# Other steps for the returns, the residual's columns, the stores and the bias tiles of an attention block, and two small moves in its opening and in its FFN

## The chip, the cores and the metric

The kernel runs on one core of a Trainium2 chip. The metric is the device time of one execution in microseconds (us). Of the kernel before, three runs were timed: 2106.54, 2106.32 and 2105.35 us, median 2106.32. One more execution was taken by the hardware profiler; the times inside the program are from it, counted from its first instruction.

## The reference, cut to what matters

One layer of a decoder on 512 tokens of width 2048, all in float32: a norm, an attention mixer, an added residual, a norm, a SwiGLU network, an added residual, a last norm.

```python
def rmsnorm(x, g):
    y = x32 * lax.rsqrt(jnp.mean(x32 * x32, axis=-1, keepdims=True) + RMS_EPS)
    return (y * g.astype(jnp.float32)).astype(x.dtype)

def nsa_mixer(h, ...):                       # 16 heads of 128 in 4 groups
    q, kc, vc, ks, vs, kw, vw, gl = jnp.split(h @ w_in, bounds, axis=-1)
    # o_c: attention on compressed keys (31 blocks), with the bias of a table by distance
    # o_s: attention on the selected blocks;  o_w: attention in a window of 512, same bias
    o = (gates[:, :, 0, :, :, None] * o_c + gates[:, :, 1, :, :, None] * o_s
         + gates[:, :, 2, :, :, None] * o_w)
    return o.reshape(Bsz, S, N_HEADS * DH) @ w_out

def swiglu(h, w_in, w_out):
    z = h @ w_in
    return (jax.nn.silu(z[..., :D_FF]) * z[..., D_FF:]) @ w_out      # D_FF = 5632

h = x
h = h + nsa_mixer(rmsnorm(h, mix_norm_g), ...)
h = h + swiglu(rmsnorm(h, ffn_norm_g), ffn_w_in, ffn_w_out)
return rmsnorm(h, final_norm_g)
```

## The kernel before, in words

**Products.** A float32 product is made of three products of a faster type, fp32r: each operand is split into a high part (a copy on ACT, the scalar engine) and a low part (a subtraction on DVE, the vector engine), and `three()` issues high·high, low·high and high·low on PE, the TensorE (lines 275 to 277). Weights come from memory into one of three `raw` buffers and are split into `whi` (L94, ACT) and `wlo` (L97, DVE).

**Opening** (0 to about 45 us). x comes in, is transposed on PE and split; the first products of the keys' weights run in four passes q = 0 to 3. The row factors of the norm (1/rms of each token) stand on a diagonal matrix `diag`; a product of an all-ones matrix with it (L516, plain float32) spreads them over all partitions, and the result scales what the projections made (`ybc`). In pass q = 0, DVE also makes sixteen small copies within `tab`, the table of biases (L498), from which POOL (GpSimd) later stores `d_c` and loads `biasc`.

**Heads** (about 200 to 710 us). A loop over h from −1 to 15 runs a stream of projections on PE, `dense()`, step by step: 32 steps for each head up to 11, 36 for heads 12 to 15. Between the steps stand events, each with a place in a table of numbers: the scores of the next head for four blocks of queries (L789 on DVE, exponentials L791 on ACT, the divisor L796 and L797 on DVE, the scaling L799 on ACT), the transposes (L804), their way through memory (`d_p`, then the `pt` fetches on SP's queue, L811), the splits of what comes back (part_hi on ACT, L831; part_lo on DVE, L845 and L847), and the products with the values (`o`). At the end of a head `fold` (L873) and `whole` (L877) add the last block, and `out_hi` (L886) and `out_lo` (L893) make the head's output. Each engine carries out its own instructions in the order in which the program gives them, so the table's numbers set the order on each engine, and an instruction that waits holds up all behind it on its engine or queue.

**Spilled heads.** The outputs of heads 0 to 10 are stored to memory (`d_o`, 256 KB each, from a `stage` buffer) at the end of their head. They come back in head iterations 11 and 12: `reload_o` (L728, SP's queue), `back_hi` (L731, ACT) and `back_lo` (L734, DVE). BACK holds the step of each reload, 9.2 + 2.7 e for the e-th; the split's halves stand 9 and 9.8 steps later. Values of 32 and more belong to iteration 12 and count from its start, in its steps (36 of them to 32 numbers).

**Partial products.** In iterations 12 to 15 the stream makes six partial products of the output projection, over heads 0 to 11, for 256 columns each: `partial(cb)`, 24 steps. It takes three blocks of weights (`W.take`, eight steps each; a take also issues the load of a later block, 512 KB, on POOL's queue, where it waits for a free `raw` buffer). The columns of x, 512 KB, are loaded into `stage` on POOL's queue (L739) at the start of the partial; at the end of steps 20 and 24 DVE adds the product's two halves to them (L752), and POOL stores the sum (`d_h`, L754).

**FFN** (from about 740 us). Blocks of the activations come back from memory: `load_form` (L1339) loads the parts from which seven combinations of a block are made, `load_a` loads blocks for the plain products (`rawx`, L1249), both on SP's queue.

Of the kernel before, what the change touches and what calls it, by code (L numbers as in the profile page):

```python
# [10 lines left out]
F32 = mybir.dt.float32  # L11
F32R = mybir.dt.float32r
# [8 lines left out]
NT, KC = S // 128, D // 128  # L21
# [158 lines left out]
def nsa_block(ctx: ExitStack, tc: tile.TileContext, x, rel_bias, mix_g, ffn_g, fin_g, w_in, w_out,  # L180
              pos_k, w1k, w2k, pos_v, w1v, w2v, f_in, f_out, onehot, out):
    nc = tc.nc
    mm, act, dve, pool = nc.tensor.matmul, nc.scalar.activation, nc.vector, nc.gpsimd
# [21 lines left out]
    d_o = dram.tile([12, 128, S], F32, name="d_o")  # L205
# [88 lines left out]
    def run(gen):  # L294
        for _ in gen:
            pass

    def split_from(psum_ap, hi, lo, scale=None):
        if scale is None:
            act(hi, psum_ap, AF.Copy)  # L300
            dve.tensor_tensor(lo, psum_ap, hi.bitcast(F32), op=OP.subtract)
        else:
            act(hi, psum_ap, AF.Copy, scale=scale)
            dve.scalar_tensor_tensor(lo, psum_ap, scale, hi.bitcast(F32), op0=OP.mult, op1=OP.subtract)
# [53 lines left out]
    with ExitStack() as st1:  # L358
# [11 lines left out]
        with ExitStack() as st0:  # L370
            xp = st0.enter_context(tc.tile_pool(name="xp", bufs=1))
# [5 lines left out]
            oh = xp.tile([NB + 1, UL], F32R, name="oh")  # L377
            ohr = xp.tile([NB + 1, UL], F32, name="ohr")
            rel_hl = [xp.tile([NB + 1, H], F32R, name=f"rel_{n}") for n in "hl"]
            ones = xp.tile([128, 128], F32, name="ones")  # L380
            diag = xp.tile([128, NT, 128], F32, name="diag")
            pool.dma_start(g16, mix_g.rearrange("o (k p) -> (o k) p", p=128))
            pool.dma_start(relt[:NB, :], rel_bias)
# [13 lines left out]
            pool.dma_start(pos[:, 1], pos_v)  # L397
            dve.memset(hn_h[:, KC - 1].bitcast(F32), 1.0)
            dve.memset(relt[NB:NB + 1, :], NEG)
            dve.memset(ones, 1.0)  # L400
            dve.memset(tab[:, UL:], NEG)

            names = iter(("tr", "mlp") * 20)
# [1 line left out]
            def bank(shape):  # L405
                return ps1.tile(shape, F32, name=next(names))
# [17 lines left out]
            def pos_turn():  # L424
                p = bank([128, 2, 32])
                for i in range(2):
                    nc.tensor.transpose(p[:, i], pos[:, i], ident[:32, :32])
                dve.tensor_copy(posT, p)

            def table(c0, c1):  # L430
                p = spare([H, 512])
                for i, r in enumerate(rel_hl):
                    mm(p[:, :c1 - c0], r, oh[:, c0:c1], start=i == 0, stop=i == 1)
                dve.tensor_copy(tab[:, c0:c1], p[:, :c1 - c0])
# [14 lines left out]
            def spare(shape):  # L449
                return ps1.tile(shape, F32, name="proj")  # L450
# [10 lines left out]
            for t in range(NT):  # L461
                if t == NT - 1:
                    p = spare([128, KC])
# [23 lines left out]
            for q in range(4):  # L487
                it = ws(ps, q, W.take(0)) if q else halves(ps)
                next(it)
                if q == 3:  # L490
                    factors()
                W.ahead(1 if q else 2)
                if q == 0:
                    for c0, c1 in ((0, 512), (512, UL)):
                        table(c0, c1)
                    pos_turn()
                    for b in range(16):
                        dve.tensor_copy(tab[:, UL + CL * b:][:, :37], tab[:, 46 - b:46 - b + 16 * 36 + 1:16])  # L498
                for i in ((0, 1), (2, 3, 4), (5, 6, 7), ())[q]:
                    square(i)  # L500
                for _ in range(4):
                    next(it)
                if q == 3:
                    W.ahead(2)
                for k in range(4 * q + 4, 4 * q + 8):
                    if q < 3:
                        chunk(k)
                    if k % 4 < 3:
                        next(it)
                run(it)  # L510
# [2 lines left out]
            for _ in range(3):  # L513
                next(kc1)
            p = bank([128, S])
            mm(p, ones, diag.rearrange("p t c -> p (t c)"), start=True, stop=True)  # L516
            act(ybc, p, AF.Copy)
            W.ahead(2)
            pool.dma_start(d_t, tab[:, :UL])
# [94 lines left out]
        for i in range(8):  # L614
# [10 lines left out]
            if i == 1:  # L625
                p = ps1.tile([128, 128], F32, name="tr")
# [27 lines left out]
        p = ps1.tile([96, G, 128], F32, name="tr")  # L654
# [8 lines left out]
    with ExitStack() as st2:  # L663
        ap_ = st2.enter_context(tc.tile_pool(name="ap", bufs=1))
# [57 lines left out]

        N_BACK = 11

        BACK = [9.2 + 2.7 * e for e in range(N_BACK)]

        def reload_o(e):
            nc.sync.dma_start(hn_l[:, e].bitcast(F32), d_o[e])  # L728
# [5 lines left out]
            dve.tensor_tensor(hn_l[:, e], hn_l[:, e].bitcast(F32), hn_h[:, e].bitcast(F32), op=OP.subtract)  # L734

        def partial(cb):
            st = ap_.tile([128, 1024], F32, name="stage").rearrange("p (t c) -> p t c", t=NT)
            c = slice(256 * cb, 256 * (cb + 1))
            pool.dma_start(st, x[:, c].rearrange("(t p) c -> p t c", p=128))  # L739
            ps = [p.rearrange("p (t c) -> p t c", t=2) for p in proj2()]  # L740
            for i in range(3):
                w = W.take()
                for t in range(NT):
                    if i == 2 and t == 2:
                        W.ahead(3)
                    for k in range(4):
                        h = 4 * i + k
                        three(ps[t // 2][:, t % 2], hn_h[:, h, tok(t)], hn_l[:, h, tok(t)], w[0][:, k], w[1][:, k],
                              h == 0 and t % 2 == 0, h == 11)
                        if h == 11 and t % 2:  # L750
                            b = t // 2
                            dve.tensor_tensor(st[:, 2 * b:2 * b + 2], st[:, 2 * b:2 * b + 2], ps[b], op=OP.add)  # L752
                            if b:
                                pool.dma_start(d_h[:, c].rearrange("(t p) c -> p t c", p=128), st)  # L754
                        if k % 2:
                            yield
# [122 lines left out]
        def out_hi(h):  # L879
            s = HS[h]  # L880
            if h < N_BACK:
                s["st"] = ap_.tile([128, 1024], F32, name="stage")[:, :S]
            f = [s["st"]] if h < N_BACK else [hn_h[:, h], hn_l[:, h]]
            s["f"] = [x.rearrange("p (t i b) -> p t i b", t=4, b=32) for x in f]
            s["o"] = s["o"].rearrange("p (i t b) -> p t i b", i=4, b=32)
            act(s["f"][0], s["o"], AF.Copy)  # L886
            if h < N_BACK:
                nc.sync.dma_start(d_o[h], s["st"])

        def out_lo(h):  # L890
            s = HS.pop(h)
# [8 lines left out]
        def steps(h):  # L900

            ev = []
            g = h + 1
            if g < H:
                for t, p in START.items():
                    p += h < 0 and t == 3
                    ev += [(p, scores, g, t), (p + 5.5, finish, g, t), (p + 8.5 - (t == 0), turn, t)]
                    if t < 3:
                        ev.append((p + 8.6 - (t == 0), fetch, t + 1))
                ev += [(p[0] + 32, f, g, 0) for p, f in ((HI, part_hi), (LO, part_lo), (VALUE, values))]  # L910
                ev.append((VALUE[0] + 33.1, fold, g))
            if h >= 0:
                ev += [(.2, load_bias, h + 2), (2.5, fetch, 0), (2.6, fetch_c)]
                for i in range(1, len(SEQ)):
                    ev += [(HI[i], part_hi, h, i), (LO[i], part_lo, h, i), (VALUE[i], values, h, i)]
                ev.append((VALUE[-1] + .5, whole, h))
                ev += [(VALUE[-1] + 1, out_hi, h), (VALUE[-1] + 2, out_lo, h)]
            for e, p in enumerate(BACK):
                for n, f in ((p, reload_o), (p + 9, back_hi), (p + 9.8, back_lo)):
                    if h == (11 if n < 32 else 12):  # L920
                        ev.append((n if n < 32 else (n - 32) * 32 / (6 * N_SPILL), f, e))
            return sorted(ev, key=lambda e: e[0])

        W.queue, W.late = pool, []
        for h in range(-1, H):
            share = 32 if h < 12 else 6 * N_SPILL
            ev = steps(h)
# [315 lines left out]
    def load_a(m):  # L1243

        for n, (home, after) in held.items():
            if after == m:
                t = tp.tile([128, 1024 if home == "rawx" else 1536], F32, name=home, bufs=1)
                a_raw[n] = t[:, :2 * S]
                nc.sync.dma_start(a_raw[n], d_a[seq[n][1]])  # L1249

    def split_a(n):
        if n in held:
            h, l = (tp.tile([128, 1600], F32R, name=f"t{x}")[:, :2 * S] for x in ("hi", "lo"))
            act(h, a_raw[n], AF.Copy)
            sub(l, a_raw.pop(n), f32(h))
            a_hl[n] = h, l
        elif n < NU - N_TAIL:
            a_hl[n] = seven[seq[n][1]] if seq[n][1] in KEPT else passing.pop(0)
        load_a(n)

    def load_tail(i):
        n = NU - N_TAIL + i
# [75 lines left out]
    def load_form(i):  # L1338
        nc.sync.dma_start(form_raw[i][:, :2], d_a[seq[forms[i]][1]].rearrange("p (n c) -> p n c", n=2))  # L1339
# [52 lines left out]
            n_visit[0] += 1  # L1392

    load_form(0)
    load_form(1)
    forming = {n: form(i) for i, n in enumerate(forms)}

# [50 lines left out]
    n, na, pending = 0, 2, None  # L1448
# [85 lines left out]
    for t in range(NT - 1):  # L1534
# [8 lines left out]
        p = known(t, 3)  # L1543
        last_columns(t, po[t], 0, 512, 3)
        send(t, factor(t, 3, p), (1,))
    t = NT - 1
# [11 lines left out]
    p = known(t, 4)  # L1558
# [4 lines left out]
    for cb, eng in ((0, nc.sync), (1, nc.scalar), (3, nc.sync), (2, nc.sync)):  # L1563
        c = slice(512 * cb, 512 * (cb + 1))
# [34 lines left out]
```

## Time and profile before

| what | value |
|---|---|
| median of three runs | 2106.32 us |
| the profiled execution's own time | 2107.27 us |
| its span, first to last instruction | 2105.5 us |
| mean granted clock of TensorE | 0.998 |
| PE busy | 2091.8 us, 99% |
| DVE, ACT, POOL busy | 1589.7, 999.9 and 142.0 us |
| PE idle at 575 to 600 us | 2.82 of 25 us |
| clock granted at 600 to 625 us | 0.93 |
| ACT waiting for d_o reloads | 4.6 us, in 2 waits |

An engine's busy time is the time in which it carried out an instruction. A timeline row gives start, length, engine, line and operation, written tile <- read tiles, and in brackets the idle time before it and what ended that. The loading of weights (PEld) overlaps with PE's products.

### The profile page before, as it was taken

How to read it: one execution, taken by the hardware profiler on the slowest of the kernel's cores; microseconds unless marked ns; L12 is line 12 of the kernel's file. 1: busy time of each engine (PE TensorE's matmuls, PEld its weight loads, DVE VectorE, ACT ScalarE, POOL GpSimd, SP SyncE). 2: the span in 40 equal slices, each digit the busy share in tenths (PEclk: the TensorE clock that was granted, in tenths of full speed). 3: DMA queues.
4: the chain of work that ended last, by engine and by line, in shares of the span. 5: the costliest groups of instructions: out<-in, count | busy, mean ns of one | idle time of the engine just before them, and what ended most of it. 6: DMA issues, size and time to landing. Idle time of an engine off the chain costs nothing.

```text
span 2105.5 us, 37607 instructions
## 1 busy us (share of the span) xinstructions
PE 2091.8 (99%) x14826; PEld 1951.9 (93%) x14826; DVE 1589.7 (75%) x2619; ACT 999.9 (47%) x1631; POOL 142.0 (7%) x230
## 2 busy tenths in 40 slices
PE   9999999999999999999999999999999999999998
PEld 7898898888989989999999999999999888999997
DVE  5565667667666467988888888888888787877776
ACT  5344666666756343444343443443434454444443
POOL 2000111111111100000000000000000000000000
PEclk9999999999999999999999999999999999999999
DMA  7555667766776753444333433443433686878884
GB/s 222 192 149 153 172 181 201 194 182 177 221 215 199 233 190 101 135 136 127 125 118 124 137 115 126 126 131 121 129 122 121 233 319 216 303 273 309 312 324 160
DMA packets 256065, 385.49 MB, mean 183 GB/s; under 512 B 27626, under 2 KB 183322, under 8 KB 255248
## 3 DMA queue, kind: packets, MB, share of 16 engines
q1 hardware_dynamic: 228832, 267.57, 40.6%
q0 software_dynamic: 26064, 113.94, 16.3%
q8 instruction: 116, 1.90, 0.4%
q10 hardware_dynamic: 992, 1.57, 0.2%
q14 instruction: 61, 0.50, 0.1%
HBM read 320.26 MB, written 68.00 MB: 184 GB/s over the span
## 4 chain that ended last, share of the span: by engine, by line
PE 94%; DMA 2%; DVE 2%; ACT 1%; issue 0%; SPq 0%; DVEq 0%; ACTq 0%
PE proj L275 14%; PE proj L276 14%; PE proj L277 14%; PE f L277 13%; PE f L275 13%; PE f L276 13%; PE pp L275 1%; PE pp L277 1%; PE pp L276 1%; DMA hn_l<-d_o 1%; PE s L277 1%; PE s L275 1%; PE s L276 1%; PE o L276 1%; PE o L277 1%; PE o L275 1%
## 5 line engine op out<-in xcount | busy, mean ns | idle before, releaser
L97 DVE TENSOR_TENSOR wlo<-raw,whi 128x1024 fp32r<-128x1024 f32 (+2 forms) x226 | 271.0, 1202 | 89.3 <-ACT whi L94 88.7
L94 ACT ACTIVATE whi<-raw 128x1024 fp32r<-128x1024 f32 (+2 forms) x226 | 233.2, 1036 | 195.7 <-DVE raw L1032 119.8
L275 PE MATMUL proj<-hn_h,whi 128*128 128x512 f32 (+1 forms) x832 | 289.1, 348 | 0.0
L276 PE MATMUL proj<-hn_l,whi 128*128 128x512 f32 (+1 forms) x832 | 287.2, 345 | 0.1
L277 PE MATMUL proj<-hn_h,wlo 128*128 128x512 f32 (+1 forms) x832 | 287.3, 345 | 0.0
L1032 DVE TENSOR_TENSOR tlo<-tt,thi 128x1536 fp32r<-128x1536 f32 (+4 forms) x161 | 197.8, 1242 | 107.7 <-ACT thi L1134 87.9
L1129 ACT ACTIVATE whi<-raw 128x1024 fp32r<-128x1024 f32 x123 | 126.1, 1057 | 292.3 <-DVE raw L1032 288.9
L277 PE MATMUL f<-hn_h,wlo 128*128 128x256 f32 x656 | 181.1, 276 | 0.0
L275 PE MATMUL f<-hn_h,whi 128*128 128x256 f32 x656 | 181.1, 276 | 0.0
L276 PE MATMUL f<-hn_l,whi 128*128 128x256 f32 x656 | 181.1, 276 | 0.0
L277 PEld LDWEIGHTS proj<-hn_h,wlo 128*128 128x128 f32 x832 | 156.2, 188 | 20.7 <-DVE wlo L97 0.2
L276 PEld LDWEIGHTS proj<-hn_l,whi 128*128 128x128 f32 x832 | 156.3, 188 | 17.8 <-DVE hn_l L417 0.5
L275 PEld LDWEIGHTS proj<-hn_h,whi 128*128 128x128 f32 x832 | 156.2, 188 | 17.0 <-issue 0.2
L277 PE MATMUL proj<-whi,hn_l 128*128 128x256 f32 (+2 forms) x568 | 163.2, 287 | 0.4 <-DVE hn_l L734 0.4
L275 PE MATMUL proj<-whi,hn_h 128*128 128x256 f32 (+2 forms) x568 | 163.1, 287 | 0.1
L276 PE MATMUL proj<-wlo,hn_h 128*128 128x256 f32 (+2 forms) x568 | 162.9, 287 | 0.0
L1134 ACT ACTIVATE thi<-tt 128x1536 fp32r<-128x1536 f32 x82 | 121.9, 1487 | 83.5 <-PE proj L276 83.4
L1032 DVE TENSOR_TENSOR wlo<-raw,whi 128x1024 fp32r<-128x1024 f32 x123 | 147.0, 1223 | 0.0
L276 PEld LDWEIGHTS f<-hn_l,whi 128*128 128x128 f32 x656 | 123.1, 188 | 0.0
L275 PEld LDWEIGHTS f<-hn_h,whi 128*128 128x128 f32 x656 | 123.1, 188 | 0.0
L277 PEld LDWEIGHTS f<-hn_h,wlo 128*128 128x128 f32 x656 | 123.1, 188 | 0.0
L275 PEld LDWEIGHTS proj<-whi,hn_h 128*128 128x128 f32 x568 | 107.2, 189 | 2.6 <-ACT hn_h L731 0.5
(378 smaller groups left out, 6225.4 us busy)
## 6 DMA issues: line engine op xcount, KB each, us to landing
raw<-in_ffn_w_in SPq DMA_DIRECT2D x135, 512.0 KB, 3.6
raw<-in_ffn_w_out SPq DMA_DIRECT2D x88, 512.0 KB, 6.1
rawx<-in_ffn_w_in SPq DMA_DIRECT2D x41, 512.0 KB, 4.8
rawx<-d_a SPq DMA_DIRECT2D x32, 512.0 KB, 5.4
ah<-d_s POOLq DMA_DIRECT2D x16, 896.0 KB, 7.2
al<-d_s POOLq DMA_DIRECT2D x16, 896.0 KB, 9.2
raw<-in_nsa_w_in POOLq DMA_DIRECT2D x24, 512.0 KB, 6.4
raw<-in_nsa_w_out POOLq DMA_DIRECT2D x24, 512.0 KB, 5.6
```

The source lines that it names most:

```text
L94: self.nc.scalar.activation(hi[:, :n], src, AF.Copy)
L97: self.nc.vector.tensor_tensor(lo[:, :n], src, hi[:, :n].bitcast(F32), op=OP.subtract)
L275: mm(o, ah, bh, start=start, stop=False, skip_group_check=True)
L276: mm(o, ah, bl, start=False, stop=False, skip_group_check=True)
L277: mm(o, al, bh, start=False, stop=stop, skip_group_check=True)
L1032: dve.tensor_tensor(o, a, b, op=OP.subtract)
L1129: act(h, r, AF.Copy)
L1134: act(h, ttf, AF.Copy)
```

## The change

What it does, piece by piece:

- Opening: `ones` becomes fp32r, `diag` is split into a high and a low part (one ACT copy, one DVE subtraction, in pass 3), and the product with the diagonal becomes two fp32r products. The sixteen copies in `tab` move from pass 0 to pass 1, behind the split of the second weights.
- Bias tiles: `load_bias` (tb, 256 KB, POOL's queue) moves from step 0.2 of a head to step 18.5.
- Spilled stores: the store of a head's output (d_o, SP's queue) moves from the end of the head to step 25.5 of the next, as `store_o`.
- Residual columns: the load of x in a partial product moves from its start to behind the second of its three takes of weights, eight steps later, and in POOL's queue behind the load that this take issues.
- Returns: the reloads' steps come from a list of their own (between 10.5 and 33, before 9.2 to 36.2), and the splits' steps too (SPLIT, between 18.6 and 42.5, before 18.2 to 45.2).
- FFN: the first `load_a(1)` moves behind `load_form(0)` on SP's queue.

```diff
-            ones = xp.tile([128, 128], F32, name="ones")
+            ones = xp.tile([128, 128], F32R, name="ones")
+            diag_hl = [xp.tile([128, NT, 128], F32R, name=f"diag_{n}") for n in "hl"]
...
                     pos_turn()
+                if q == 1:
                     for b in range(16):
                         dve.tensor_copy(tab[:, UL + CL * b:][:, :37], tab[:, 46 - b:46 - b + 16 * 36 + 1:16])
...
                 if q == 3:
                     W.ahead(2)
+                    split_from(diag, *diag_hl)
...
             p = bank([128, S])
-            mm(p, ones, diag.rearrange("p t c -> p (t c)"), start=True, stop=True)
+            for i, d in enumerate(diag_hl):
+                mm(p, ones, d.rearrange("p t c -> p (t c)"), start=i == 0, stop=i == 1)
...
-        BACK = [9.2 + 2.7 * e for e in range(N_BACK)]
+        BACK = [10.5, 12, 13.5, 17.2, 18.4, 19.6, 20.8, 25.6, 26.6, 27.6, 33]
+        SPLIT = [18.6, 19.8, 21.2, 25.8, 27, 28.2, 30.5, 34, 36, 39, 42.5]
...
         def partial(cb):
-            st = ap_.tile([128, 1024], F32, name="stage").rearrange("p (t c) -> p t c", t=NT)
             c = slice(256 * cb, 256 * (cb + 1))
-            pool.dma_start(st, x[:, c].rearrange("(t p) c -> p t c", p=128))
             ps = [p.rearrange("p (t c) -> p t c", t=2) for p in proj2()]
             for i in range(3):
                 w = W.take()
+                if i == 1:
+                    st = ap_.tile([128, 1024], F32, name="stage").rearrange("p (t c) -> p t c", t=NT)
+                    pool.dma_start(st, x[:, c].rearrange("(t p) c -> p t c", p=128))
...
             if h < N_BACK:
-                nc.sync.dma_start(d_o[h], s["st"])
+                spilled[h] = s["st"]
+
+        spilled = {}
+
+        def store_o(h):
+            nc.sync.dma_start(d_o[h], spilled.pop(h))
...
             if h >= 0:
-                ev += [(.2, load_bias, h + 2), (2.5, fetch, 0), (2.6, fetch_c)]
+                ev += [(18.5, load_bias, h + 2), (2.5, fetch, 0), (2.6, fetch_c)]
...
-            for e, p in enumerate(BACK):
-                for n, f in ((p, reload_o), (p + 9, back_hi), (p + 9.8, back_lo)):
+            if 0 < h <= N_BACK:
+                ev.append((25.5, store_o, h - 1))
+            for e, (p, q) in enumerate(zip(BACK, SPLIT)):
+                for n, f in ((p, reload_o), (q, back_hi), (q + .8, back_lo)):
...
-        load_a(n)
+        if n != 1:
+            load_a(n)
...
     load_form(0)
+    load_a(1)
     load_form(1)
```

What the tables do to the order is seen in the engines' instruction lists. First DVE at the end of head 11, from the fold to the next head's scores. L873, L877 and L893 are fold, whole and out_lo before (L879, L883 and L904 after); hn_l<-hn_l,hn_h is the low part of a returned head (L734, then L739). Before:

```order
L873 TENSOR_REDUCE p_1868<-s 128x128
L877 TENSOR_TENSOR o<-o,p_1868 128x4x32
L734 TENSOR_TENSOR hn_l<-hn_l,hn_h 128x512
L893 TENSOR_TENSOR hn_l<-o,hn_h 128x512
L327 SCALAR_TENSOR_TENSOR yt<-proj,ybc 128x512
L301 TENSOR_TENSOR ql<-yt,qh 128x512
L97 TENSOR_TENSOR wlo<-raw,whi 128x1024
L734 TENSOR_TENSOR hn_l<-hn_l,hn_h 128x512
```

After:

```order
L879 TENSOR_REDUCE p_1873<-s 128x128
L739 TENSOR_TENSOR hn_l<-hn_l,hn_h 128x512
L883 TENSOR_TENSOR o<-o,p_1873 128x4x32
L904 TENSOR_TENSOR hn_l<-o,hn_h 128x512
L327 SCALAR_TENSOR_TENSOR yt<-proj,ybc 128x512
L301 TENSOR_TENSOR ql<-yt,qh 128x512
L739 TENSOR_TENSOR hn_l<-hn_l,hn_h 128x512
L97 TENSOR_TENSOR wlo<-raw,whi 128x1024
```

A returned head's low part moved from behind whole to ahead of it, and another from behind the weights' low part to ahead of it.

Then DVE some 5 us later, from the scores of a block of queries to its divisor (L796 and L797, then L802 and L803) and the next block's scores. Before:

```order
L789 ISA p_1869,ms<-s,tb 128x16x32
L789 ISA ms 128x1
L734 TENSOR_TENSOR hn_l<-hn_l,hn_h 128x512 x2
L796 RECIPROCAL ms<-ms 128x3
L797 TENSOR_TENSOR ms<-ms,gates 128x3
L734 TENSOR_TENSOR hn_l<-hn_l,hn_h 128x512
L789 ISA p_1868,ms<-s,biasc 128x31
```

After:

```order
L795 ISA p_1874,ms<-s,tb 128x16x32
L795 ISA ms 128x1
L739 TENSOR_TENSOR hn_l<-hn_l,hn_h 128x512 x3
L802 RECIPROCAL ms<-ms 128x3
L803 TENSOR_TENSOR ms<-ms,gates 128x3
L795 ISA p_1873,ms<-s,biasc 128x31
```

Three low parts now stand ahead of the divisor, where two stood ahead and one behind.

Last, POOL's queue in iterations 12 to 14, where raw are the loads of weights, stage the columns of x, tb a bias tile and d_h the store of a partial product. Before:

```order
L739 DMA stage<-in_x 128x4x256
L673 DMA tb<-d_u 128x512
L78 DMA raw<-in_nsa_w_out 128x4x256 x3
L754 DMA d_h<-stage 128x4x256
L739 DMA stage<-in_x 128x4x256
L78 DMA raw<-in_nsa_w_out 128x4x256
L673 DMA tb<-d_u 128x512
```

After:

```order
L748 DMA stage<-in_x 128x4x256
L78 DMA raw<-in_nsa_w_out 128x4x256 x2
L677 DMA tb<-d_u 128x512
L760 DMA d_h<-stage 128x4x256
L78 DMA raw<-in_nsa_w_out 128x4x256
L748 DMA stage<-in_x 128x4x256
L78 DMA raw<-in_nsa_w_out 128x4x256 x2
```

The second load of x stands behind one more load of weights, and the bias tile ahead of the store of the partial product.

More of the change, by code (lines that the diff above doesn't have):

```diff
@@ L399, in nsa_block @@
             dve.memset(relt[NB:NB + 1, :], NEG)
-            dve.memset(ones, 1.0)
+            dve.memset(ones.bitcast(F32), 1.0)
             dve.memset(tab[:, UL:], NEG)
```

## The prediction

> **What bounds the kernel now.** I read the page first, for the busy shares, then the windows of 25 us, to find where TensorE is not busy, then waits, chain and timelines of those places. In a row of the windows stand the stretch, its length, then busy time and count of PE, PEld, DVE, ACT and POOL, the granted clock, the DMA share and GB/s.
>
> ```profile
> PE 2091.8 (99%) x14826; PEld 1951.9 (93%) x14826; DVE 1589.7 (75%) x2619; ACT 999.9 (47%) x1631; POOL 142.0 (7%) x230
> 0.00:25.00 25.00, 23.31 (x114) 18.53 (x115) 13.45 (x38) 15.39 (x26) 6.97 (x18) 1.00 0.90 295
> 575.00:600.00 25.00, 22.18 (x143) 18.90 (x141) 19.05 (x45) 17.24 (x41) 2.79 (x4) 1.00 0.88 238
> 600.00:625.00 25.00, 24.43 (x180) 23.78 (x181) 16.68 (x44) 12.41 (x33) 5.04 (x7) 0.93 0.61 200
> 1650.00:1675.00 25.00, 24.36 (x128) 20.63 (x127) 22.54 (x38) 13.79 (x20) 1.60 (x3) 1.00 0.79 280
> ```
>
> TensorE is the bound. Every window not shown has 25.00 of 25 us busy, but for the last stage; so a step moved elsewhere can only lose. The one large loss lies at 575 to 625, where heads 11 and 12 meet. Three stretches with the same work, iterations 12, 13 and 14 of the heads' loop, price it:
>
> ```profile
> 581.90:621.40 39.50, 36.26 (x265) 34.14 (x264) 28.76 (x74) 23.23 (x57) 6.35 (x9) 0.96 0.71 207
> 621.40:654.00 32.60, 32.60 (x265) 32.02 (x264) 20.48 (x59) 18.80 (x48) 5.73 (x9) 1.00 0.67 194
> ```
>
> 39.50 − 32.60 = 6.9 us. Inside iteration 12 the loss sits in one spot:
>
> ```profile
> 600.38 0.45 PE L276 MATMUL o<-pt_hl,v1h 128*128 128x256 f32 x1 [2.13 <-DVE pt_hl L845]
> 598.00:600.00 2.00, 0.25 (x3) 0.04 (x1) 0.97 (x2) 1.41 (x4) 0.00 (x0) 1.00 1.13 222
> 602.00:604.00 2.00, 2.00 (x11) 2.00 (x11) 0.10 (x1) 0.63 (x1) 0.76 (x1) 0.51 0.22 77
> ```
>
> TensorE waited 2.13 us for a low part on DVE (L845), and then ran at half clock for a while: by the 0.93 granted over 600 to 625, 0.07 × 25 = 1.7 us more. That is 3.8 of the 6.9.
>
> [...]
>
> **Returns and their splits.** Heads 0 to 10 come back from memory (the d_o reloads) and are split by ACT (L731) and DVE (L734). The waits seem to accuse the reloads: ACT lost 0.79 us at the ninth, 3.83 at the eleventh.
>
> ```profile
> 593.43 0.63 ACT L731 ACTIVATE hn_h<-hn_l 128x512 fp32r<-128x512 f32 x1 [0.79 <-DMA hn_l<-d_o]
> 593.97 1.54 ACT L799 ACTIVATE p<-p,ms 128x31 f32<-128x31 f32 x3
> 603.24 0.63 ACT L731 ACTIVATE hn_h<-hn_l 128x512 fp32r<-128x512 f32 x1 [3.83 <-DMA hn_l<-d_o]
> PE proj L277 <- DVE hn_l L734: 0.4, 2, 0.2
> ```
>
> (The last row is from the waits of TensorE at 555 to 606: total, times, longest.) The change sends the last reloads earlier, the ninth and tenth ahead of the heads' turn, the eleventh 3.2 steps sooner and so ahead of the pt fetches of step 2.5; I expect both waits to go. What that is worth is read from DVE, in whose order L845 stands:
>
> ```profile
> 592.15 1.29 DVE L734 TENSOR_TENSOR hn_l<-hn_l,hn_h 128x512 fp32r<-128x512 f32 x2 [1.50 <-ACT hn_h L731]
> 593.57 0.16 DVE L797 TENSOR_TENSOR ms<-ms,gates 128x3 f32<-128x3 f32 x1
> 599.03 0.69 DVE L734 TENSOR_TENSOR hn_l<-hn_l,hn_h 128x512 fp32r<-128x512 f32 x1 [1.81 <-ACT hn_h L731]
> 599.64 0.69 DVE L845 TENSOR_TENSOR pt_hl<-pt,pt_hl 128x512 fp32r<-128x512 f32 x1
> ```
>
> L845 waits for the L734 ahead of it, that for ACT's split (1.81), that for the exponentials ahead of it on ACT, and these for L799, which could have begun when L797 ended, at 593.73, and began at 593.97 behind the late split. So the 0.79 us held L845 back by 0.24. The 3.83 us was mostly idle: L845 had gone, and TensorE's two waits for such a split are 0.4 in all. Both together: 0.6 us.
>
> Against that, the new order puts one split's low part ahead of L877. It stood behind it, in the time in which ACT makes out_hi, and cost nothing; now its 0.6 (1.29 for two) and out_hi (0.6 for that shape on ACT, at 593.43) are paid one after the other, less the 0.1 that DVE waited: yt and the next scores come up to 1.1 later. And three low parts stand ahead of L797 where two stood: another 0.6. The split at the place just ahead of L845 stays (now the eleventh, before the tenth). So L845 would end up to 1.1 + 0.6 − 0.2 = 1.5 us later. In favour: the reloads no longer compete with the pt fetches, two splits less are left to iteration 12, and the stalls before (6.9 − 3.8 − 0.4 = 2.7 us) may shrink by about as much. I take **0**, with +1.5 as the bad end and −6.9, all of the loss, as the good one. The half clock stays in the sum, since a gap of 2 us stays.
>
> **The residual's columns (x).** The load of x (512 KB) for a partial product stood at its start; it now goes behind the first take's weights in POOL's queue. Where DVE adds it (L752), all that is behind on DVE waits with it. Partial 1 (GB/s is that of 40 slices of 618 to 634, the rows under it the DMA issues there with the time to landing):
>
> ```profile
> 620.84 0.75 POOL L739 DMA_DIRECT2D stage<-in_x  x1 [5.54 <-DMA d_h<-stage]
> 622.96 0.75 POOL L78 DMA_DIRECT2D raw<-in_nsa_w_out  x1 [1.36 <-issue]
> GB/s 412 403 424 351 332 434 426 425 302 288 257 198 162 238 280 300 341 353 210 113 228 243 197 179 220 243 302 302 210 216 288 252 168 156 113 36 184 389 297 297
> stage<-in_x POOLq DMA_DIRECT2D x1, 512.0 KB, 6.0
> tb<-d_u POOLq DMA_DIRECT2D x1, 256.0 KB, 8.7
> 628.46 0.69 DVE L752 TENSOR_TENSOR stage<-stage,proj 128x512 f32<-128x512 f32 x1 [2.66 <-PE proj L277]
> 632.35 0.69 DVE L752 TENSOR_TENSOR stage<-stage,proj 128x512 f32<-128x512 f32 x1 [0.72 <-PE proj L277]
> 634.33 0.65 DVE L845 TENSOR_TENSOR pt_hl<-pt,pt_hl 128x512 fp32r<-128x512 f32 x1
> 635.10 0.32 PE L276 MATMUL o<-pt_hl,v1h 128*128 128x256 f32 x1
> ```
>
> x would be issued at 623.7, where tb stood. If it flies 6.0 us as now, it lands at 629.7, 1.2 after it is wanted; if 8.7, like tb, at 632.4, 3.9 late. DVE can take up 0.72 (its idle before the second add) and 0.12 (634.98 to 635.10). TensorE's stall: 0.4 to 3.1; I take the middle, **+1.75**. Partial 4 stands alike:
>
> ```profile
> 688.16 0.70 POOL L78 DMA_DIRECT2D raw<-in_nsa_w_out  x1 [1.04 <-issue]
> 692.31 0.69 DVE L752 TENSOR_TENSOR stage<-stage,proj 128x512 f32<-128x512 f32 x1 [4.71 <-PE proj L277]
> 695.03 0.69 DVE L752 TENSOR_TENSOR stage<-stage,proj 128x512 f32<-128x512 f32 x1 [0.90 <-PE proj L277]
> 695.64 0.69 DVE L845 TENSOR_TENSOR pt_hl<-pt,pt_hl 128x512 fp32r<-128x512 f32 x1
> 697.67 0.28 PE L276 MATMUL o<-pt_hl,v1h 128*128 128x256 f32 x1
> ```
>
> Issued at 688.9, by 6.0 us it lands at 694.9, 2.6 late, by 8.7 at 697.6, 5.3 late; the slack is 0.90 + 1.34 = 2.24. Stall 0.4 to 3.1; no tb fetch crowds it, so nearer the low end: **+0.8**. The other four partials fall between fetch bursts: 0.
>
> [...]
>
> **The opening.** Sixteen small copies held DVE while TensorE wanted L417:
>
> ```profile
> 16.48 1.67 DVE L498 COPY tab<-tab 16x37 f32<-16x37 f32 x16
> PEld proj L276 <- DVE hn_l L417: 0.5, 1, 0.5
> 25.33 0.75 DVE L417 SCALAR_TENSOR_TENSOR hn_l<-mlp,gcol,hn_h 128x512 fp32r<-128x512 f32 x1 [2.75 <-ACT hn_h L416]
> 40.66 0.39 PE L277 MATMUL proj<-hn_h,wlo 128*128 128x512 f32 x1
> 40.89 1.02 PE L516 MATMUL mlp<-diag,ones 128*128 128x512 f32 x2
> 41.98 0.39 PE L276 MATMUL proj<-hn_l,whi 128*128 128x512 f32 x1
> ```
>
> Behind the second weights they fall into 2.75 us of DVE idleness, which hides their 1.67: **−0.4** (0.5 less what PEld hides). Without that cover they would cost the same again. The fp32 product (two rows of L516, and with one matmul behind them 40.89 to 41.98, 1.09 us) becomes two of fp32r; three matmuls at 0.23 a start (40.66 to 40.89) are 0.69: **−0.4**. The diagonal's split adds one ACT copy and one DVE subtraction of 512 columns, 0.6 to 0.7 each by the rows above, while TensorE works through the last matmuls ahead of 40.89; if it is late, up to +0.5.
>
> **The row factor, FFN.** A reload (rawx) stood ahead of the form's data (acc) on SP:
>
> ```profile
> 1652.41 0.43 DVE L1035 TENSOR_TENSOR acc<-acc 128x256 f32<-128x256 f32 x1 [0.75 <-DMA acc<-d_a]
> 1662.90 0.39 PE L277 MATMUL f<-thi,al 128*128 128x256 f32 x1 [0.64 <-DVE al L1032]
> ```
>
> With acc first, DVE's 0.75 goes and the chain down to L1032 moves up: the 0.64 and some of the next start, **−0.7** (0 if rawx, now behind, is late in its turn).
>
> **Bias tiles and spilled stores.** tb moves from step 0.2 to 18.5, the d_o store from the head's end to step 25.5 of the next; each has several us until it is wanted, and in iterations 0 to 10 TensorE never waits. Cover gone, a late store would block the stage buffer of the next head: I price it at 0, bound +1.
>
> **The sum.** The profiled execution took 2107.27 us (span 2105.5). 0 + 1.75 + 0.8 − 0.4 − 0.4 − 0.7 = +1.05, so 2108.3; that execution lies 0.95 above the runs' median of 2106.32, so **2107.4** among the runs. 0.2% (4.2 us) is about what a measurement of this kernel can tell from no change: faster is below 2102.1, slower above 2110.5.
>
> **The rivals.**
> 1. *The splits were the whole loss* (faster). Sent early and taken in one batch, they leave ACT and DVE free, the wait at L845 falls well under 2 us and the half clock stays away. For it: no other iteration loses anything, and what iteration 12 has beyond 13 is the splits. Against: four of them still stand there, one just ahead of L845. −6.9 − 1.5 = 2106.3 − 8.4 = 2097.9; without the half clock alone, −1.7 − 1.5 and some 1.5 of stall: 2101.6. Chance 0.25.
> 2. *x comes late* (slower). Its place is the add in partials 1 and 4; it decides from about 1 us above my middle, x later than 632 and 697. 3.1 + 3.1 − 1.5 = +4.7 → 2111.0, with a half clock behind one of the stalls (+1.7) 2112.7. For it: transfers issued there now fly 6.0 to 8.7 us. Chance 0.25.
> 3. *x is in time, the returns even out*: −1.5 alone, 2104.8. Chance 0.17.
> My forecast 0.33. Should the store or the diagonal be late, the time stays within these.
>
> **The range**: 2100.5, which leaves out the full gain of the first rival (about 0.12), to 2111.5, which leaves out the worst half of the second (0.08). Faster 0.26 (all of the first rival, a sliver of the third), slower 0.24, within 0.2% 0.50.
>
> **What would show it.** Right: ACT has no wait for d_o; L845 of iteration 12 still makes TensorE wait about 2 us with clock 0.5 behind it; the chain shows stage<-in_x ahead of L752 near 630 and 695; the windows at 0 and 1650 gain 0.8 and 0.7. Wrong: iteration 12 near 33 us, or L752 waiting for PE alone.

## The result and the profile after

| kernel | median | lowest to highest | runs |
|---|---|---|---|
| before | 2106.07 us | 2105.21 to 2106.87 | 6 |
| changed | 2118.12 us | 2115.29 to 2119.82 | 6 |

The ratio is 1.0057, with a 95% interval of 1.0044 to 1.007: 12 us slower, well beyond the 0.2% that count as a difference here. The forecast was 2107.4, the range 2100.5 to 2111.5; the time lies outside it.

The profiled execution of the changed kernel took 2119.57 us (span 2117.9). The windows of 25 us show where the time went. Columns as before: stretch, length, busy time and count of PE, PEld, DVE, ACT, POOL, then clock, DMA share, GB/s.

```profile
575.00:600.00 25.00, 21.22 (x141) 18.60 (x139) 18.19 (x43) 16.30 (x36) 1.50 (x2) 1.00 0.86 235
600.00:625.00 25.00, 23.52 (x175) 23.07 (x176) 16.16 (x42) 11.97 (x32) 5.76 (x8) 0.93 0.55 187
625.00:650.00 25.00, 22.69 (x172) 22.16 (x171) 13.55 (x46) 15.08 (x42) 2.28 (x4) 0.93 0.58 167
650.00:675.00 25.00, 22.47 (x166) 21.58 (x166) 12.58 (x35) 11.51 (x27) 4.27 (x6) 0.93 0.72 210
675.00:700.00 25.00, 25.00 (x207) 24.69 (x207) 15.20 (x40) 13.61 (x33) 5.20 (x7) 1.00 0.65 206
700.00:725.00 25.00, 22.76 (x186) 22.25 (x185) 9.29 (x13) 6.08 (x9) 3.66 (x5) 1.00 0.54 164
```

Of these stretches, the kernel before lost time between 575 and 625 only: TensorE idled 2.82 + 0.57 us and lost 0.07 × 25 = 1.75 us by the clock, 5.1 in all. Now it idles 3.78 + 1.48 + 2.31 + 2.53 + 2.24 = 12.3 us, and three windows instead of one have a clock of 0.93, 5.25 us. That is 17.6, or 12.5 more than before. Of it 10.6 (7.1 idle, 3.5 clock) stand behind 625, and 1.9 at 575 to 625.

TensorE's waits from 550 to 720 us name what it waited for (total, times, longest):

```profile
PE o L276 <- DVE pt_hl L851: 6.5, 3, 3.0
PE s L275 <- DVE p L879: 2.9, 2, 2.5
PE o L275 <- ACT pt_hl L837: 1.1, 1, 1.1
PE o L276 <- DVE pt_hl L853: 1.0, 1, 1.0
```

L851 is the low part that was L845, L879 is fold. Three of these stalls stand right behind an add of x (L758, L752 before) on DVE, in partials 1, 2 and 4 (counted from 0). Partial 1, DVE's timeline:

```profile
632.63 0.69 DVE L758 TENSOR_TENSOR stage<-stage,proj 128x512 f32<-128x512 f32 x1 [6.27 <-issue]
635.73 0.68 DVE L758 TENSOR_TENSOR stage<-stage,proj 128x512 f32<-128x512 f32 x1
637.70 0.65 DVE L851 TENSOR_TENSOR pt_hl<-pt,pt_hl 128x512 fp32r<-128x512 f32 x1
```

The first add came after 6.27 us of idleness; "issue" means that the profile assigns it to no releaser, but x, issued at 624.27, took 8.3 us and landed at about 632.6, when the add began. From there DVE worked without a gap, and TensorE waited 1.06 us at 636.77 and 1.25 us at 638.40. Partial 2 and partial 4, DVE's timeline first:

```profile
660.39 0.69 DVE L758 TENSOR_TENSOR stage<-stage,proj 128x512 f32<-128x512 f32 x1 [7.23 <-DMA stage<-in_x]
662.52 0.38 DVE L879 TENSOR_REDUCE p<-s 128x128 f32<-128x256 f32 x1
...
706.22 0.69 DVE L758 TENSOR_TENSOR stage<-stage,proj 128x512 f32<-128x512 f32 x1 [9.40 <-issue]
```

and TensorE's behind it:

```profile
662.96 0.40 PE L275 MATMUL s<-k1h,qh 128*128 128x288 f32 x1 [2.53 <-DVE p L879]
...
709.30 0.39 PE L276 MATMUL o<-pt_hl,v1h 128*128 128x256 f32 x1 [2.24 <-DVE pt_hl L851]
```

In partial 2 it is not the values' low part but fold that stands behind the late add, and TensorE's next scores wait for fold. POOL's queue shows why x is late:

```profile
623.53 0.75 POOL L78 DMA_DIRECT2D raw<-in_nsa_w_out  x1 [5.83 <-issue]
624.27 0.75 POOL L748 DMA_DIRECT2D stage<-in_x  x1
...
650.82 0.75 POOL L78 DMA_DIRECT2D raw<-in_nsa_w_out  x1 [9.17 <-DVE wlo L97]
651.56 0.75 POOL L748 DMA_DIRECT2D stage<-in_x  x1
```

The load of x goes out right behind a load of weights, ahead of which POOL idled 5.83 us (no releaser named) and 9.17 us, the latter until DVE freed a buffer (wlo, L97). Against the kernel before, x goes out 3.4 us later in partial 1 (624.27, before 620.84) and 8.4 in partial 2 (651.56, before 643.14). On ACT, the waits for d_o are gone from the list, as expected.

### The profile page after: what moved, and what is told of

The parts are those of the page before. It is cut to its first block, busy times and chain, and to the rows that moved or that the text cites. A ratio compares the mean times of both kernels' runs of the same rounds, so it can differ in the third digit from the quotient of the medians.

```text
span 2117.9 us, 37607 instructions
## 1 busy us (share of the span) xinstructions
PE 2094.8 (99%) x14826; PEld 1954.2 (92%) x14826; DVE 1589.1 (75%) x2620; ACT 1001.0 (47%) x1632; POOL 141.8 (7%) x230
## 4 chain that ended last, share of the span: by engine, by line
PE 91%; DMA 3%; DVE 2%; ACT 2%; issue 1%; SPq 0%; POOL 0%; DVEq 0%; ACTq 0%; POOLq 0%
PE f L276 13%; PE f L277 13%; PE f L275 13%; PE proj L275 13%; PE proj L276 13%; PE proj L277 13%; DMA pt<-d_p 1%; PE pp L275 1%; PE pp L276 1%; PE pp L277 1%; PE s L277 1%; PE s L275 1%; PE s L276 1%; PE o L276 1%; PE o L277 1%
## 5 line engine op out<-in xcount | busy, mean ns | idle before, releaser
L97 DVE TENSOR_TENSOR wlo<-raw,whi 128x1024 fp32r<-128x1024 f32 (+2 forms) x226 | 271.4, 1203 | 89.1 <-ACT whi L94 88.7
L276 PE MATMUL proj<-hn_l,whi 128*128 128x512 f32 (+1 forms) x832 | 287.2, 345 | 0.0
L276 PE MATMUL f<-hn_l,whi 128*128 128x256 f32 x656 | 181.1, 276 | 0.0
L276 PEld LDWEIGHTS proj<-hn_l,whi 128*128 128x128 f32 x832 | 156.3, 188 | 17.4 <-DVE hn_l L418 0.3
L276 PE MATMUL proj<-wlo,hn_h 128*128 128x256 f32 (+2 forms) x568 | 163.8, 288 | 0.0
L276 PEld LDWEIGHTS f<-hn_l,whi 128*128 128x128 f32 x656 | 123.2, 188 | 0.0
L805 ACT ACTIVATE p<-p,ms 128x31 f32<-128x31 f32 (+2 forms) x192 | 78.6, 472 | 74.5 <-DVE ms L803 74.5
```

The lines of the kernel that those rows point to most:

```text
L97: self.nc.vector.tensor_tensor(lo[:, :n], src, hi[:, :n].bitcast(F32), op=OP.subtract)
L276: mm(o, ah, bl, start=False, stop=False, skip_group_check=True)
L805: act(p, p, AF.Copy, scale=r[:, i:i + 1])
```

## The experiments

The theory after the result (A): x comes late in partials 1, 2 and 4 and costs about 11 us; the returns cost about 1 us by the order on DVE; the rest is small. Rivals: the later stalls are a consequence of the returns (B); ACT's waits for the reloads were the loss of the kernel before (C); bias tiles or stores cost something (D). Each kernel was timed beside the kernel before on the same chip. That one's median was 2106.06 us beside four of them (x put back, x alone, the returns alone, without x and returns) and 2106.59 beside the others.

**x put back.** The changed kernel, with

```diff
         def partial(cb):
+            st = ap_.tile([128, 1024], F32, name="stage").rearrange("p (t c) -> p t c", t=NT)
             c = slice(256 * cb, 256 * (cb + 1))
+            pool.dma_start(st, x[:, c].rearrange("(t p) c -> p t c", p=128))
...
-                if i == 1:
-                    st = ap_.tile([128, 1024], F32, name="stage").rearrange("p (t c) -> p t c", t=NT)
-                    pool.dma_start(st, x[:, c].rearrange("(t p) c -> p t c", p=128))
```

> The changed kernel with the load of x put back to the start of each partial product; all else as changed. Theory A (x comes late, everything else is small): the three stalls in partials 1, 2 and 4 (2.75 + 2.7 + 2.4 us in the trace of the changed kernel) and the two half-clock spells behind them (2 x 1.7) go, so 2118.1 - 11.3 = about 2107, within 1 us of before plus what the returns cost (+1.2) less the opening (-0.6). Rival B (the returns' new order pushes iteration 12, and the later stalls are its consequence): the stalls at 635, 660 and 707 stay in part, 2112 or more.

Measured: 2107.13 us (2105.0 to 2108.33, 10 runs), ratio to before 1.0001 (0.9991 to 1.001). The stretch from 625 on is whole again:

```profile
625.00:650.00 25.00, 25.00 (x204) 24.60 (x202) 16.85 (x53) 17.86 (x48) 4.31 (x6) 1.00 0.67 198
```

So are 650 to 675 and 700 to 725; 575 to 600 still has TensorE busy for 21.23 of 25 us. Theory A holds, B falls: with the returns as changed the later stalls are gone.

**x alone moved.** The kernel before, with only the change's move of x.

> The kernel before with only the load of x moved behind the second take. Theory A: the stalls of partials 1, 2 and 4 appear here too, 2106.1 + 11 = about 2117; DVE waits for stage<-in_x at L752 there, 5 to 9 us each. Rival B: x alone is hidden, 2106 to 2108.

Measured: 2116.03 us (2115.96 to 2119.83), ratio 1.0048 (1.0033 to 1.0063): 10 us slower. DVE's waits from 600 to 720 us:

```profile
DVE stage L753 <- issue: 15.0, 2, 9.2
DVE stage L753 <- DMA stage<-in_x: 10.6, 3, 6.9
```

and two windows:

```profile
625.00:650.00 25.00, 23.24 (x173) 22.57 (x173) 14.10 (x44) 15.60 (x42) 3.33 (x5) 0.93 0.53 154
650.00:675.00 25.00, 22.86 (x172) 22.09 (x172) 13.02 (x35) 10.52 (x26) 2.88 (x5) 0.93 0.70 206
```

L753 is the add of x. By these rows DVE idled 10.6 us ahead of it for x and 15.0 more with no releaser named (as in partial 1 above); the kernel before idled ahead of it 19.6 us, all of it for TensorE's products. The move of x is the loss; in the kernel before it costs 10 us, where theory A had 11.

**Same step, other place in the queue.** The changed kernel, with x at the second take, but ahead of it:

```diff
             for i in range(3):
-                w = W.take()
                 if i == 1:
                     st = ap_.tile([128, 1024], F32, name="stage").rearrange("p (t c) -> p t c", t=NT)
                     pool.dma_start(st, x[:, c].rearrange("(t p) c -> p t c", p=128))
+                w = W.take()
```

> The changed kernel with the load of x at the same step (the second take), but ahead of that take's load of weights in POOL's queue instead of behind it. Theory A1 (x is late because it stands behind a load that waits for a free buffer, and then flies behind it): x goes out 2 to 10 us sooner, the stalls of partials 1, 2 and 4 go, about 2107, as with x at the start. Theory A2 (eight steps later is too late in any place, since the fetches crowd it): 2113 or more.

Measured: 2107.46 us (2106.47 to 2108.49), ratio 1.0004 (0.9995 to 1.0013). POOL's queue in this kernel, partials 1 and 2:

```profile
622.93 0.76 POOL L747 DMA_DIRECT2D stage<-in_x  x1 [6.54 <-DVE wlo L97]
623.68 0.75 POOL L78 DMA_DIRECT2D raw<-in_nsa_w_out  x1
...
643.78 0.75 POOL L747 DMA_DIRECT2D stage<-in_x  x1 [4.92 <-DMA d_h<-stage]
646.58 0.75 POOL L78 DMA_DIRECT2D raw<-in_nsa_w_out  x1 [2.05 <-DVE wlo L97]
```

In partial 1 x goes out only 1.3 us sooner than in the changed kernel (622.93 against 624.27), but it now takes 4.8 us instead of 8.3: SP's fetches fly as before (2.19 MB on its queue from 618 to 634 us, 2.35 in the changed kernel), but no other load of its own queue flies just ahead of it. In partial 2 it goes out at 643.78 instead of 651.56, since it no longer waits for a `raw` buffer (some 4 us of that difference, 2.3 + 1.75, are the delay that partial 1 had brought the changed kernel). So the eight steps cost nothing that the times can tell; the place behind the weights costs 11 us.

**The returns alone.** The kernel before, with the new BACK and SPLIT lists.

> The kernel before with only the new steps of reloads and splits. Theory A (from the order on DVE and ACT: one low part more ahead of whole and one more ahead of the divisor): the waits for d_o go, but TensorE's wait for the low part ahead of the values grows from 2.1 to about 3 us; 2106.1 + 1.2 = about 2107.3. Rival C (the reloads' waits were the loss): iteration 12 falls from 39.5 towards 33 us, 2099 to 2102.

Measured: 2107.47 us (2106.96 to 2108.37), ratio 1.0005 (0.9995 to 1.0014). The medians differ by 1.4 us, as theory A has it, but the interval holds 1, so a loss is not shown by the times alone. Rival C's gain is not seen, though the new order could hide it; the next run takes the reloads alone. The waits of TensorE from 550 to 720 us say what the list did:

```profile
PE o L276 <- DVE pt_hl L846: 3.0, 1, 3.0
PE o L276 <- DVE pt_hl L848: 1.0, 1, 1.0
PE s L275 <- DVE ms L790: 0.6, 1, 0.6
PE s L275 <- DVE p L874: 0.4, 1, 0.4
PE proj L277 <- DVE hn_l L735: 0.2, 1, 0.2
```

ACT waits for d_o no more (its list of waits has none), and TensorE's wait at the values grew from 2.1 to 3.0 us.

**The reloads alone, splits at their old steps.**

```diff
-        BACK = [9.2 + 2.7 * e for e in range(N_BACK)]
+        BACK = [10.5, 12, 13.5, 17.2, 18.4, 19.6, 20.8, 25.6, 26.6, 27.6, 33]
+        SPLIT = [18.2 + 2.7 * e for e in range(N_BACK)]
```

> The kernel before with the new steps of the eleven reloads, the splits at their old steps. ACT's waits for d_o go. Theory A (those waits held TensorE by 0.24 and 0.4 us only): 2105.4, TensorE still waits about 2 us for the low part L845 with a half-clock spell behind it. Rival C (the waits were the loss): 2099 to 2102.

Measured: 2106.17 us (2103.72 to 2107.2), ratio 0.9996 (0.9986 to 1.0005): no change that the times can tell, and rival C is out. ACT has no wait for d_o, and TensorE still waits:

```profile
PE o L276 <- DVE pt_hl L846: 2.1, 1, 2.1
PE s L275 <- DVE p L874: 0.6, 1, 0.6
PE proj L277 <- DVE hn_l L735: 0.2, 1, 0.2
```

Its window behind that wait:

```profile
600.00:625.00 25.00, 25.00 (x202) 24.55 (x203) 16.90 (x46) 14.15 (x37) 5.05 (x7) 1.00 0.65 206
```

Taking the 4.6 us of ACT's waits away took 0.2 us off TensorE's. In this execution, the fastest of the ten, no half clock followed the 2.1 us.

**Without x and without the returns' steps.** The changed kernel with both undone; opening, bias tiles and stores are left.

> The changed kernel without the move of x and without the new steps of reloads and splits: opening, bias tiles and stores are left (the FFN's edit leaves the order of the instructions as it was). Theory A: only the opening's 0.6 to 0.8 us are left, 2105.4. Rival D (bias tiles or stores at their new steps cost something): 2107 or more.

Measured: 2105.24 us (2103.79 to 2106.99), ratio 0.9994 (0.9985 to 1.0004). D is not seen, though a cost of 1 us would not show either; the medians give 0.8 us of gain, the interval holds 1.

**The opening alone.** Both of its edits on the kernel before.

> The kernel before with only the two edits of the opening (copies behind the second weights; the diagonal's split and two products). Theory A: both gains of 0.4 us are there, 2106.3 - 0.8 = about 2105.5. Rival (the diagonal's low part comes late, or the bias tiles and stores made the 0.8 us that were seen with all three): 2106.0 or more.

Measured: 2105.47 us (2105.05 to 2107.87, 11 runs), ratio 0.9996 (0.9987 to 1.0005). The median is where theory A puts it, but the traces bear out only one of the two gains. The product with the diagonal, in this run:

```profile
40.68 0.39 PE L520 MATMUL mlp<-diag_h,ones 128*128 128x512 f32 x1
41.36 0.39 PE L276 MATMUL proj<-hn_l,whi 128*128 128x512 f32 x1
```

From the product to this L276 it is 0.68 us, against 1.09 before (40.89 to 41.98): that is the 0.4 us of the two fp32r products, and all eight traces with this edit have it. The copies' 0.4 us is in none. The product began at 40.58 to 40.89 us in the four traces with the copies in pass 0, and at 40.61 to 40.98 in the eight with the copies moved. The low part for which TensorE waited 0.5 us (L417, now L418) still makes it wait 0.5 us here. So the agreement of the median with theory A is luck in part.

**The splits spread anew.** Opening, bias tiles and stores as changed, x at the start of each partial, new reloads, and the halves of the splits in lists of their own:

```diff
+        SPLIT = [18.2, 18.9, 19.5, 23.6, 26.3, 28, 29.2, 31, 41.3, 41.6, 41.9]
+        LOW = [19, 19.7, 22.7, 25.75, 27.1, 29.5, 31.3, 34, 43.7, 44.5, 45.2]
...
-                for n, f in ((p, reload_o), (q, back_hi), (q + .8, back_lo)):
+                for n, f in ((p, reload_o), (q, back_hi), (r, back_lo)):
```

> Opening, bias tiles and stores as changed, x at the start of each partial, reloads at the new steps, and the splits spread anew: the low parts of heads 8, 9 and 10 behind the low part that the values wait for (L845 of iteration 12) instead of ahead of it, that of head 5 behind whole again, that of head 2 behind the low part of its block. Theory A (the order on DVE and ACT ahead of L845 is what is paid): the 2 to 3 us wait and its half-clock spell go, iteration 12 falls from 39.5 to 33 to 35 us, 2105.2 - 5 = about 2100. Rival E (the pt fetches land too late for L845 in any order): the wait stays over 1.5 us, 2103.5 or more.

Measured: 2100.97 us (2100.8 to 2101.77), ratio 0.9974 (0.9964 to 0.9984). The wait at the values is gone, and so is the half clock, by the windows (the third row is the values' low part on DVE):

```profile
575.00:600.00 25.00, 23.39 (x164) 21.34 (x163) 20.16 (x47) 17.46 (x41) 3.00 (x4) 1.00 0.88 250
600.00:625.00 25.00, 25.00 (x201) 24.42 (x201) 16.09 (x46) 14.12 (x38) 4.28 (x6) 1.00 0.77 235
593.88 0.69 DVE L851 TENSOR_TENSOR pt_hl<-pt,pt_hl 128x512 fp32r<-128x512 f32 x1
```

L851 follows the transposes at once. In the changed kernel it began at 600.74, behind the low part of a returned head, which itself waited 2.02 us for ACT's copy.

TensorE's waits from 550 to 720 us that are left:

```profile
PE proj L277 <- DVE hn_l L740: 1.1, 1, 1.1
PE s L275 <- DVE p L879: 0.4, 1, 0.4
```

The order on DVE and ACT was the loss: x put back has the same reloads and the same place of x, and took 2107.13 us. Whether the old reloads would have allowed this order was not run.

**The same with x at the second take, ahead of it.**

> As the spread splits, and the load of x at the second take, ahead of that take's load of weights. If A1 holds, x is in time, and its 512 KB no longer compete with the pt fetches of 585 to 595: the same as the spread splits or up to 1 us less, 2099 to 2100. If A2 holds, 6 us or more above the spread splits.

Measured: 2101.31 us (2100.89 to 2103.0), ratio 0.9973 (0.9964 to 0.9983). The same as without, within 0.3 us; taking x out of the burst at 590 is worth nothing that the times can tell once L851 is off the path.

**The two waits that were left.** Head 4's low part behind whole, heads 6 and 7 behind the first scores, heads 8 and 9 copied by ACT ahead of these and finished right behind L851:

```diff
-        SPLIT = [18.2, 18.9, 19.5, 23.6, 26.3, 28, 29.2, 31, 41.3, 41.6, 41.9]
-        LOW = [19, 19.7, 22.7, 25.75, 27.1, 29.5, 31.3, 34, 43.7, 44.5, 45.2]
+        SPLIT = [18.2, 18.9, 19.5, 23.6, 26.3, 28, 29.2, 31, 32.4, 32.5, 41.3]
+        LOW = [19, 19.7, 22.7, 25.75, 29.5, 31.3, 34, 34.1, 43.7, 43.8, 44.5]
```

> As the spread splits (x at the start of each partial), with what its trace still shows taken out: the splits of heads 8 and 9 on ACT ahead of the next head's scores, so that both low parts can follow the low part L845's values wait for, and head 4's low part behind whole. TensorE's wait of 1.1 us for a returned head and that of 0.4 us for fold go. Theory A: 2101.0 - 1.5 to 2 = about 2099.2. Rival (DVE is simply full there and the wait moves to another place): 2100.5 or more.

Measured: 2099.09 us (2098.46 to 2099.27, 5 runs), ratio 0.9963 (0.9951 to 0.9975): 7 us faster than the kernel before, 19 us faster than the changed one, and below both in every run. TensorE is left with 0.45 us of idleness at 575 to 600, by the window:

```profile
575.00:600.00 25.00, 24.55 (x177) 23.07 (x176) 21.64 (x56) 18.88 (x44) 3.01 (x4) 1.00 0.92 264
```

and with one wait:

```profile
PE s L275 <- DVE ms L795: 0.4, 1, 0.4
```

## Why the prediction was wrong

**The residual's columns: right mechanism, wrong size.** This is the step that failed. The term was +2.55 us (1.75 + 0.8 + 0); the move costs 10 (alone) to 11 us (taken back). The 7.5 to 8.5 us beyond the term are most of the 10.7 us between forecast and time; the rest is the returns' 1.4 and gains of 1.1 that did not come. Three parts of the term were mis-sized.

- The flight. I put it between 6.0 and 8.7 us and took the middle. It was 8.3 in partial 1, 8.7 in partial 2 and 8.1 in partial 4: near the upper end each time. There x flew behind the weights of its own queue and beside 0.65 to 1.45 MB of SP's transfers, as tb did in the kernel before (8.7 us), and tb's row was the one to take, not the middle. In partials 0 and 3, where SP moved less than 0.4 MB meanwhile, x took 6.1 and 5.3 us behind the weights. In partial 1 the weights and x took 9.1 us together: from 623.5 us to the landing at 632.6 the DMA engines moved 2.52 MB, 277 GB/s, and POOL's queue had 1.05 MB of it, half of what was moved until 628.6, a quarter from there on. TensorE idled there 1.06 + 1.25 = 2.3 us where the term had 1.75, in partial 4 2.24 where it had 0.8.
- "The other four partials fall between fetch bursts: 0." Partial 2 cost 2.53 us of idleness. There POOL idled 9.17 us ahead of the weights, until a buffer was free, and behind the late add stood fold, for which TensorE's scores wait. I had followed only one consumer behind the add, the low part of the values, and never asked in which partial another stands there.
- The half clock. I kept it as an extra of rival 2, once. It came twice, behind the stalls of partials 1 and 2, 1.75 us each. The stalls were over 2 us (1.06 + 1.25 and 2.53), as was the one ahead of it in the kernel before (2.13); behind partial 4's 2.24 us it did not come (the last section has the lengths). Without half clock the move costs most of its price all the same: the one execution of the changed kernel without such a spell (by its mean clock of 0.999, see the last section) took 2115.29 us.

By these, rival 2 was the case that came true: its mechanism, its place in partials 1 and 4, its decisive point (x later than 632: it landed at 632.6). Its worst price was 2112.7; what it lacked is partial 2 with its half clock (4.3) and the returns' 1.2 to 1.4. That these sum to the 2118 is luck in part: it had 6.2 us for the stalls of partials 1 and 4, where 4.55 was seen, and it counted 1.1 us of gains, from the copies and the FFN, that did not come.

**The returns: the working was right, the choice was not.** The chain through L734, ACT's split, the exponentials and L799 gave up to +1.5 us for L845, with the 0.24 from the reloads' waits already taken off. I set that to 0 on the ground that the stalls ahead "may shrink by about as much". They did not: idleness at 575 to 600 went from 2.82 to 3.78 us, and the wait at the values from 2.13 to 2.96 us. The low part (L845, then L851) came 1.1 us later. The medians give +1.4 for the returns alone, though the times by themselves don't prove it. That the waits for d_o were not the loss is shown: with the reloads early and the splits where they were, the time stays.

**Rival 1** (the splits were the whole loss) had the right cause and the wrong kernel: the splits' order was worth 4 to 6 us against the old steps (2105.24, then 2100.97 and 2099.09 with the spread ones), 6 to 8 against the list of the change (2107.13 with x put back), but only with the low parts put behind the one that TensorE waits for. The list of the change put three of them and one more ahead of it.

**The row factor of the FFN: the edit moves nothing.** `load_a(1)` issues no transfer, so SP's instructions stand in the same order as before. The −0.7 was argued from a row that the edit cannot touch. That it might do nothing was not weighed, and the order of SP's instructions would have shown it. TensorE's idleness went from 0.64 us at 1662 to 0.15 us between 1650 and 1700 in the changed kernel, and 0.7 us appeared at 1716; neither can come from this edit.

**The opening.** The product's −0.4 is there, the copies' −0.4 is not. The row of L516 is gone in the changed kernel, but the low part L418 still makes TensorE's weight loads wait (0.4 and 0.3 us), and its window at 0, which was to gain 0.8 us, has 23.14 of 25 us busy, before 23.31. The medians give 0.8 us (with bias tiles and stores) and 1.1 us (alone), against −0.8 predicted; both intervals hold 1, and the traces show half of it.

**Bias tiles and stores**: priced at 0, and nothing that the times can tell is seen.

## What to carry to other kernels

The adds of x held up all that stood behind them on DVE: it idled 6.27, 7.23 and 9.40 us ahead of them in partials 1, 2 and 4, and TensorE idled 2.3, 2.53 and 2.24 us behind them. So before a transfer is moved, list in every place where it occurs what its queue waits for ahead of it, and which consumers stand behind its reader. A transfer that flew behind another of its queue, beside another queue's burst, was to be priced here by the last one of such a burst (8.1 to 8.7 us), not by its usual flight (4 to 6 in partials 1 to 5 of the kernel before). And where a waiting instruction is blamed for a stall, ask when it would have begun without the wait: here 4.6 us of waits on transfers held TensorE by 0.2, and it was the order behind them that paid, 4 to 6 us, once the low parts stood behind the one that TensorE wanted.

## What was not expected of the hardware

In these profiles the half clock did not go by the length of a stall alone. Where the wait at the values was 3.0 us, in the changed kernel, with x put back, with the returns alone and with x ahead of the take, a window of 0.93 followed in all four profiles. Between 2.1 and 2.8 us it went both ways: before, a window of 0.93 followed on 2.13 us, and with x alone on 2.2 us; with the reloads alone none followed on 2.1 us, with x and returns back none on 2.2 us, with the opening alone none on 2.8 us. In the changed kernel one followed on 2.53 us (partial 2) and on 1.06 and 1.25 us close together (partial 1), none on 2.24 us (partial 4).

The spell in the kernel before, a row of the windows, and the wait with the opening alone, with the window behind it:

```profile
600.55:603.97 3.42, 3.42 (x17) 3.42 (x18) 0.97 (x2) 0.63 (x1) 0.76 (x1) 0.50 0.29 95
```

```profile
PE o L276 <- DVE pt_hl L849: 2.8, 1, 2.8
600.00:625.00 25.00, 23.21 (x180) 22.36 (x181) 16.81 (x44) 12.45 (x33) 5.04 (x7) 1.00 0.64 202
```

The three spells of the changed kernel were as long: 0.50 was granted from 602.27 to 605.69 us, from 639.82 to 643.24 and from 663.71 to 667.13. Half of 3.42 us is the 1.7 us that each cost by the windows. By the lengths alone it can't be told which stall a spell will follow: 2.1 and 2.2 us stand on both sides.

What a spell costs in the end varies too. The mean clock is on record for every timed execution; in eleven profiles, by their windows between 575 and 725 us, 0.999 goes with no window of 0.93, 0.998 with one, 0.996 or 0.997 with three. With the reloads alone the three executions at 0.999 took 2103.72 to 2105.04 us, the seven at 0.998 took 2106.08 to 2107.2. But of the kernel before, timed beside them, ten at 0.999 and eighteen at 0.998 have medians of 2106.45 and 2106.6 us, and x alone took 2116.01 us in its one execution at 0.999, as much as in two of its three at 0.996 (2115.96 and 2116.05). Other idleness took the place of the spell with the opening alone: TensorE idled 3.50 + 1.79 us at 575 to 625, before 2.82 + 0.57. By these numbers I estimate the price of a stall of 2 to 3 us in this kernel with 0 to 1.7 us on top, and one that is removed may give back more than its length, as with the spread splits: 2107.13 us with x put back, where the longest wait was 3.0 us, and 2100.97 with them.
